# The token factor behind the gate and up matmuls, the shift as one more input column, in the last half FFN

## The chip, the cores and the metric

One core of a Trainium2 chip. TensorE does the matmuls, VectorE (DVE) and ScalarE (ACT) the elementwise work, GpSimd (POOL) some of it, SyncE (SP) starts the transfers. The metric is the device time of one execution in microseconds (us).

## The reference

Two blocks on 256 tokens of width 1024, in float32. The second has two layers; the last step of its second layer is a half FFN on the 256 latent tokens alone. In short:

```python
def half_ffn(t, m, j):
    h = modulate(rmsnorm_2(t, norm_g[l, j]), m[3 * j], m[3 * j + 1])
    return t + 0.5 * m[3 * j + 2] * swiglu(h, w_gate, w_up, w_down)

def rmsnorm_2(x, g):   # per token: x * rsqrt(mean(x * x) + eps) * g
def modulate(h, shift, scale):  return h * (1 + scale) + shift
def swiglu(h, w_gate, w_up, w_down):  return (silu(h @ w_gate) * (h @ w_up)) @ w_down
```

With r the token's factor rsqrt(mean(x * x) + eps), s = g * (1 + scale) per channel and b the shift per channel, the input is h = r * (x * s) + b. So h @ w = r * ((x * s) @ w) + (b @ w): a factor per token, and a constant per output channel. The FFN is 2816 wide. Ahead of it stands the retention layer, which ends with an output projection that is added to x.

## The kernel before, in words

Activations lie transposed: 128 channels on the partitions, tokens along the free axis, eight channel blocks (KB) for the width of 1024. Every float32 product is made of three matmuls on numbers rounded to fp32r (`mm3`, L488 to L491): high weight by high input, high weight by the input's rest, the weight's rest by high input. So each weight tile and each input has a high part and a rest (`wh`, `wl`; `hh`, `ho`; `ah`, `ao`).

Weights come in items of 1 MB by DMA into `raw`, and are split in units: ScalarE casts to `wh` (L388), VectorE subtracts to `wl` (L389). `Stream.get` (L404) hands out the next unit and then calls `ahead` (L400), which splits on until two units wait (AHEAD, L332); with `later=True` it does not. `wh` and `wl` have four buffers each.

The order is the program's: every engine takes its instructions as the code issues them (`manual_schedule`), so a split that `get` issues stands on ScalarE and VectorE between the elementwise work before and after it.

The retention's output projection (L1738 to L1755) runs in two halves of eight output blocks m. Each block is 24 matmuls of 256 columns, then a residual step on VectorE (L1750). In the second half ScalarE squares the new block (`square`, L662 to L671) and GpSimd or VectorE adds up the squares. After block 7 come the column sums (`norm_s`, L677 and L678), the factor (`norm_v`: L581 on VectorE, the power of -0.5 on GpSimd, L582), two transposes to get it along the free axis (`norm_b`, L694) and the copy to `Rb` (L701).

The last FFN is `ffn(1, 2, 1, None)`, one lane of N = 256 tokens. Its `start` makes the first two of its output blocks: for each channel block k `norm_u` (L710, `hu` = x * s * Rb) on VectorE, the shift and the split in `norm_h` (L722 to L727) on ScalarE, VectorE and GpSimd, and gate and up interleaved behind it. The other blocks go gate, then up: 24 matmuls each, Silu from PSUM on ScalarE (`act_in`, L1273), the product with up from PSUM on VectorE (`av`, L1278), the cast `ah` on ScalarE (L1279), the rest `ao` on VectorE (L1280). The FFN's width goes in two halves h of 11 blocks, 22 units each for gate and up; after each half the down projection: eight blocks of 33 matmuls, in units of 6 and 5 tiles (768 and 640 columns), each with a residual (L1353). PSUM has four banks (`pj`) for all of this.

Of the kernel before, what the change touches and what calls it, by code (L numbers as in the profile page):

```python
# [445 lines left out]
def build(tc, aps, stage=99):  # L446
# [4 lines left out]
    with ctx:  # L451
# [36 lines left out]
        def mm3(out, wh, wl, xh, xlo, first, last):  # L488
            pe.matmul(out, wh, xh, start=first, stop=False)  # L489
            pe.matmul(out, wh, xlo, start=False, stop=False)  # L490
            pe.matmul(out, wl, xh, start=False, stop=last)  # L491
# [188 lines left out]
        def norm_s(a):  # L680
            Z["ps", a] = ps = bank("at", "pss")
            sums(ps, 0, Z["ss"][:, LANE[a]], Z["sq", a])
# [20 lines left out]
        def norm_b(a):  # L703
            norm_t(a)
            norm_c(a)
# [552 lines left out]
        def ffn(l, j, lanes, nxt, first=0, ready=(), on_k=None, first_s=None, post=None):  # L1258
            N = 256 * lanes
            FF = ExitStack()  # L1260
            qp = FF.enter_context(tc.tile_pool(name=f"ffn{l}{j}", bufs=1, reuse_waits="tile"))
            if lanes == 1:
                skew = qp.tile([128, 48], F32, name="skew")
                pool.memset(skew, 0.0)
                Z["hh"] = qp.tile([128, KB, N], F32R, name="h1")
                Z["ho"] = qp.tile([128, KB, N], F32R, name="o1")
            hh, ho, gx = Z["hh"], Z["ho"], Z["gx"]
            ah = qp.tile([128, 11, N], F32R, name="ah")
            ao = qp.tile([128, 11, N], F32R, name="ao")

            def act_in(pg):
                sg = qp.tile([128, N], F32, name="sg", tag="sg", bufs=2)
                act.activation(sg, pg[:, :N], AF.Silu)  # L1273
                return sg

            def act_out(m, sg, pu):
                av = qp.tile([128, N], F32, name="av", tag="av", bufs=2)
                dve.tensor_tensor(av, sg, pu[:, :N], op=OP.mult)  # L1278
                act.copy(ah[:, m, :], av)  # L1279
                dve.tensor_tensor(ao[:, m, :], av, ah[:, m, :].bitcast(F32), op=OP.subtract)  # L1280

            def start():
                order = [first, 1 - first][:lanes]
                w, ps = [], [[bank("pj") for _ in range(2)] for _ in range(2)]
                done = {a: KB if a in ready else 0 for a in range(2)}
                done[0] = Z.pop("prep", 0)

                def prepare(a, k):
                    while done[a] <= min(k, KB - 1):
                        norm_h(l, j, done[a], a, first_s, a or done[a] % 2)  # L1290
                        done[a] += 1

                prepare(order[0], 1)
                for i, a in enumerate(order):
                    L = LANE[a]
                    for m in range(2):
                        if i == 0:
                            w.append([W.get(("gu", l, j, m), later=True) for _ in range(2)])
                        span = 1
                        for u, k in [(u, k0 + k) for k0 in range(0, KB, span) for u in range(2) for k in range(span)]:  # L1300
                            if m == u == 0:
                                prepare(a, k + 2)
                            s = slice(k * 128, (k + 1) * 128)
                            wh, wl = w[m][u]
                            mm3(ps[m][u][:, L], wh[:, s], wl[:, s], hh[:, k, L], ho[:, k, L], k == 0, k == KB - 1)
                            if u == 0:
                                continue
                            step = 8 * m + k
                            if i == 0 and lanes == 2:
                                if on_k:  # L1310
                                    on_k(step)
                                if step > 11:
                                    prepare(order[1], step - 12)
                            if i == 0 and step in ((2, 5) if lanes == 2 else (4, 7)) and len(W.split) < 2:
                                W.split_next()
                        if i == len(order) - 1:
                            act_out(m, act_in(ps[m][0]), ps[m][1])
                            if m == 0:
                                W.split_next()
                                W.split_next()  # L1320
                            else:
                                W.ahead()
                                if first_s:
                                    th.spawn(first_x())
                        if i or m or lanes == 1:
                            th.tick()

            for h in range(2):
                for m in range(11):
                    if h == 0 and m < 2:  # L1330
                        if m == 0:
                            start()
                        continue
                    key = ("gu", l, j, h * 11 + m)
                    for u in range(2):
                        wh, wl = W.get(key)
                        ps = bank("pj")
                        for k in range(KB):
                            s = slice(k * 128, (k + 1) * 128)
                            mm3(ps[:, :N], wh[:, s], wl[:, s], hh[:, k, :N], ho[:, k, :N], k == 0, k == KB - 1)  # L1340
                        if u == 0:
                            sg = act_in(ps)
                        else:
                            act_out(m, sg, ps)
                        th.tick()
# [203 lines left out]
        def retention():  # L1549
# [186 lines left out]
            derive_gate(1, 1)  # L1736
            derive_scale(1, 2)
            gh, go = G2["h"], G2["o"]  # L1738
            for khalf in range(2):
                if khalf == 1:  # L1740
                    th.drain()
                for m in range(KB):
                    wh, wl = W.get(("ro", khalf, m // 2), later=(khalf == 1 and m > KB - 3))
                    o = bank("pj")[:, :T]
                    for i in range(8):
                        s = slice(i * 128, (i + 1) * 128)
                        k = 8 * khalf + i
                        mm3(o, wh[:, s], wl[:, s], gh[:, k, :], go[:, k, :], i == 0, i == 7)
                    x = xl[:, m, :]
                    dve.scalar_tensor_tensor(x, o, gx[:, 1, 1, m, 0:1], x, op0=OP.mult, op1=OP.add)  # L1750
                    if khalf == 1:
                        square(m, 0)
                        if m == KB - 2:
                            W.split_next()
                    th.tick()  # L1755
            norm_s(0)
            norm_v(0)
            W.ahead()
            norm_b(0)
            RC.close()  # L1760
            RB.close()

# [53 lines left out]
```

## Time and profile before

| | |
|---|---|
| median of 3 runs | 2265.23 us (2263.64 to 2265.62) |
| the profiled execution | 2270.17 us, span 2268.4 us |
| TensorE matmuls, busy in the span | 2231.9 us (98%) |
| VectorE, ScalarE, GpSimd | 1428.7 (63%), 919.4 (41%), 179.2 us (8%) |
| mean granted TensorE clock | 0.995 |
| from the last output matmul of the retention to the end | from 2060.9 to 2268.4 us |

Times in the rows are us from the start of the span. A row of a group gives line, engine, operation, tiles (out<-in), shapes and count, then busy time and the mean ns of one, and what ended the idle time before. A row of the order in time gives start, duration, the same names, and in brackets the engine's idle time before and what ended it. PE is TensorE; a granted clock of 1.00 is 2.4 GHz.

### The profile page before, as it was taken

Reading aid. Unit: us, or ns where it says so; the run is one execution under the profiler, and the core shown is the slowest. Engines: PE = TensorE matmul, PEld = TensorE weight load, DVE = VectorE, ACT = ScalarE, POOL = GpSimd, SP = SyncE. Lnnn points to the kernel's source line nnn. Section 1 sums busy time; section 2 is a strip of 40 time slices with the busy share of each in tenths; the row PEclk is TensorE's granted clock in tenths of the full one; section 3 lists DMA queues with packets and bytes.
Section 4 is the critical chain, followed back from the end, with each engine's and each line's share of the span. In section 5 each row is a group of like instructions: output and inputs, shape, how many; then the busy total and the mean of one; then the engine's idle time right before and its main releaser. Section 6 shows DMA issues by size and latency. Waiting matters only on the chain.

```text
span 2268.4 us, 30969 instructions
## 1 busy us (share of the span) xinstructions
PE 2231.9 (98%) x12576; PEld 1907.8 (84%) x12576; DVE 1428.7 (63%) x2160; ACT 919.4 (41%) x1453; POOL 179.2 (8%) x207
## 2 busy tenths in 40 slices
PE   9999999999999999999999999999999999999998
PEld 7787887878888887898888888888888888899998
DVE  6776667766577766555666566556555656665554
ACT  5455444556432333454322334332232533335443
POOL 2100011012100000111000002000001100001001
PEclk9999999999999999999999999999999999999999
DMA  6444565445344554212445444344434423344553
GB/s 238 139 140 140 184 233 194 172 149 186 135 176 169 196 181 150 103 65 104 167 162 181 170 150 155 121 140 157 148 127 146 150 103 124 137 161 164 177 197 110
DMA packets 57167, 351.67 MB, mean 155 GB/s; under 512 B 6464, under 2 KB 6976, under 8 KB 23872
## 3 DMA queue, kind: packets, MB, share of 16 engines
q1 hardware_dynamic: 55872, 346.02, 43.5%
q10 hardware_dynamic: 1152, 3.67, 0.5%
q8 instruction: 98, 1.61, 0.3%
q14 instruction: 45, 0.37, 0.0%
HBM read 348.62 MB, written 1.05 MB: 154 GB/s over the span
## 4 chain that ended last, share of the span: by engine, by line
PE 87%; DVE 5%; ACT 3%; issue 2%; DMA 1%; POOL 1%; SPq 0%; DVEq 0%; ACTq 0%; POOLq 0%
PE pj L489 20%; PE pj L490 20%; PE pj L491 20%; PE pj L640 4%; PE pj L641 3%; PE pj L642 3%; DVE wl L389 2%; PE pj L1605 1%; PE pj L1607 1%; PE pj L1606 1%; ACT wh L388 1%; PE psc L933 1%; PE ada L527 1%; PE ppv L1061 1%; DMA raw<-w 1%
## 5 line engine op out<-in xcount | busy, mean ns | idle before, releaser
L389 DVE TENSOR_TENSOR wl<-raw,wh 128x1024 fp32r<-128x1024 f32 (+4 forms) x549 | 621.0, 1144 | 333.1 <-ACT wh L388 331.9
L388 ACT CAST wh<-raw 128x1024 fp32r<-128x1024 f32 (+4 forms) x549 | 520.7, 967 | 235.4 <-DMA raw<-w 145.6
L490 PE MATMUL pj<-ho,wh 128*128 128x512 f32 (+1 forms) x1280 | 465.6, 364 | 3.4 <-POOL ho L727 1.8
L489 PE MATMUL pj<-hh,wh 128*128 128x512 f32 (+1 forms) x1280 | 467.4, 365 | 0.5 <-ACT hh L722 0.4
L491 PE MATMUL pj<-hh,wl 128*128 128x512 f32 (+1 forms) x1280 | 464.3, 363 | 0.8 <-DVE wl L389 0.8
L489 PEld LDWEIGHTS pj<-hh,wh 128*128 128x128 f32 x1280 | 241.4, 189 | 45.6 <-ACT sg L1273 5.0
L516 DVE SCALAR_TENSOR_TENSOR acc<-raw,sc,acc 128x1024 f32<-128x1024 f32 x224 | 278.9, 1286 | 0.0
L490 PEld LDWEIGHTS pj<-ho,wh 128*128 128x128 f32 x1280 | 241.5, 189 | 42.8 <-POOL ho L727 3.4
L491 PEld LDWEIGHTS pj<-hh,wl 128*128 128x128 f32 x1280 | 241.5, 189 | 39.2 <-DVE wl L389 1.0
L489 PE MATMUL pj<-ah,wh 128*128 128x512 f32 (+1 forms) x770 | 268.7, 349 | 0.3 <-ACT wh L388 0.3
L491 PE MATMUL pj<-ah,wl 128*128 128x512 f32 (+1 forms) x770 | 266.8, 347 | 0.5 <-DVE wl L389 0.5
L490 PE MATMUL pj<-ao,wh 128*128 128x512 f32 (+1 forms) x770 | 266.7, 346 | 0.0
L640 PE MATMUL pj<-wh,xh 128*128 128x512 f32 (+2 forms) x480 | 191.4, 399 | 0.0
L641 PE MATMUL pj<-wl,xh 128*128 128x512 f32 (+2 forms) x480 | 184.7, 385 | 2.9 <-DVE wl L389 2.9
L642 PE MATMUL pj<-wh,xo 128*128 128x512 f32 (+2 forms) x480 | 183.7, 383 | 0.0
L1279 ACT CAST ah<-av 128x512 fp32r<-128x512 f32 (+1 forms) x88 | 49.9, 567 | 313.9 <-DVE av L1278 313.9
L489 PEld LDWEIGHTS pj<-ah,wh 128*128 128x128 f32 x770 | 145.0, 188 | 24.1 <-ACT wh L388 4.7
L491 PEld LDWEIGHTS pj<-ah,wl 128*128 128x128 f32 x770 | 145.8, 189 | 19.5 <-DVE wl L389 1.1
L490 PEld LDWEIGHTS pj<-ao,wh 128*128 128x128 f32 x770 | 145.1, 188 | 17.6
L670 POOL TENSOR_TENSOR ss<-ss,sq 128x256 f32<-128x256 f32 x55 | 48.6, 891 | 1308.6 <-ACT sq L668 1308.4
L1278 DVE TENSOR_TENSOR av<-sg,pj 128x512 f32<-128x512 f32 (+1 forms) x88 | 54.6, 620 | 149.5 <-PE pj L491 135.3
L1273 ACT ACTIVATE sg<-pj 128x512 f32<-128x512 f32 (+1 forms) x88 | 47.8, 543 | 192.8 <-PE pj L491 192.6
(316 smaller groups left out, 3468.9 us busy)
## 6 DMA issues: line engine op xcount, KB each, us to landing
raw<-w SPq DMA_DIRECT2D x258, 1024.0 KB, 4.8
raw<-w SPq DMA_DIRECT2D x64, 704.0 KB, 4.1
raw<-w SPq DMA_DIRECT2D x16, 768.0 KB, 4.2
de<-decay SPq DMA_DIRECT2D x24, 256.0 KB, 4.5
raw<-w SPq DMA_DIRECT2D x4, 904.0 KB, 4.5
raw<-w SPq DMA_DIRECT2D x6, 512.0 KB, 3.7
mk<-masks ACTq DMA_DIRECT2D x2, 768.0 KB, 5.1
xl<-xt SPq DMA_DIRECT2D x4, 256.0 KB, 5.4
```

The costliest lines, as they stand in the source:

```text
L388: self.nc.scalar.copy(hi[:, d], r[:, o])
L389: (sub or self.nc.vector).tensor_tensor(lo[:, d], r[:, o], hi[:, d].bitcast(F32), op=OP.subtract)
L489: pe.matmul(out, wh, xh, start=first, stop=False)
L490: pe.matmul(out, wh, xlo, start=False, stop=False)
L491: pe.matmul(out, wl, xh, start=False, stop=last)
L516: dve.scalar_tensor_tensor(acc[:, r, :], w, s, acc[:, r, :], op0=OP.mult, op1=OP.add)
L640: pe.matmul(o, xh[:, k, ts], wh[:, s], start=(k == 0), stop=False)
L641: pe.matmul(o, xh[:, k, ts], wl[:, s], start=False, stop=False)
L642: pe.matmul(o, xo[:, k, ts], wh[:, s], start=False, stop=(k == KB - 1))
L670: (dve if k == KB - 2 else pool).tensor_tensor(d, d, q, op=OP.add)
L1278: dve.tensor_tensor(av, sg, pu[:, :N], op=OP.mult)
L1279: act.copy(ah[:, m, :], av)
```

## The change

Only the FFN with one lane changes. `hh` is now x * s alone, made block by block in the retention's second output half (`act.activation` with the scale, and the rest `ho` on VectorE), in the middle 256 columns (48 to 304) of the tiles that the two-lane FFNs use. Two more columns (304, 305) hold the shift, so that each of the 1056 gate and up matmuls has 258 columns. `late` takes each result from PSUM: `nt` is the result times `Rb`, `nb` the column of the shift. Gate: Silu of `nt` with `nb` as bias. Up: (`nt` + `nb`) * Silu in one VectorE step. `start` isn't called for one lane any more: all blocks go gate, then up. The norm's sums and factor are issued after the first gate (`norm_r(0)`), the transposes and the copy to `Rb` after the first up (`norm_b(0)`); the gate result waits in its bank until then. In the retention the two places that held splits back (`later`) or issued them by hand are gone.

```diff
             if lanes == 1:
                 skew = qp.tile([128, 48], F32, name="skew")
                 pool.memset(skew, 0.0)
-                Z["hh"] = qp.tile([128, KB, N], F32R, name="h1")
-                Z["ho"] = qp.tile([128, KB, N], F32R, name="o1")
-            hh, ho, gx = Z["hh"], Z["ho"], Z["gx"]
+                hh, ho = hh[:, :, 48:306], ho[:, :, 48:306]
+            NI = hh.shape[-1]
...
+            def late(ps):
+                t = qp.tile([128, N], F32, name="nt", tag="nt", bufs=3)
+                b = qp.tile([128, 1], F32, name="nb", tag="nb", bufs=4)
+                dve.tensor_tensor(t, ps[:, :N], Z["Rb"][:, :N], op=OP.mult)
+                dve.tensor_copy(b, ps[:, N:N + 1])
+                return t, b
+
             def act_in(pg):
                 sg = qp.tile([128, N], F32, name="sg", tag="sg", bufs=2)
-                act.activation(sg, pg[:, :N], AF.Silu)
+                if lanes == 1:
+                    t, b = late(pg)
+                    act.activation(sg, t, AF.Silu, bias=b)
+                else:
+                    act.activation(sg, pg[:, :N], AF.Silu)
                 return sg
 
             def act_out(m, sg, pu):
                 av = qp.tile([128, N], F32, name="av", tag="av", bufs=2)
-                dve.tensor_tensor(av, sg, pu[:, :N], op=OP.mult)
+                if lanes == 1:
+                    t, b = late(pu)
+                    dve.scalar_tensor_tensor(av, t, b, sg, op0=OP.add, op1=OP.mult)
+                else:
+                    dve.tensor_tensor(av, sg, pu[:, :N], op=OP.mult)
...
-                    if h == 0 and m < 2:
+                    if h == 0 and m < 2 and lanes == 2:
...
-                            mm3(ps[:, :N], wh[:, s], wl[:, s], hh[:, k, :N], ho[:, k, :N], k == 0, k == KB - 1)
+                            mm3(ps[:, :NI], wh[:, s], wl[:, s], hh[:, k], ho[:, k], k == 0, k == KB - 1)
+                        if lanes == 1 and h == m == 0:
+                            if u == 0:
+                                norm_r(0)
+                                pg = ps
+                                continue
+                            norm_b(0)
+                            sg = act_in(pg)
...
             gh, go = G2["h"], G2["o"]
+            X = slice(48, 304)
+            for i in (304, 305):
+                act.copy(hh[:, :, i:i + 1], mods[:, 1, 48:56, 0:1])
+                dve.tensor_tensor(ho[:, :, i:i + 1], mods[:, 1, 48:56, 0:1], hh[:, :, i:i + 1].bitcast(F32),
+                                  op=OP.subtract)
...
-                    wh, wl = W.get(("ro", khalf, m // 2), later=(khalf == 1 and m > KB - 3))
+                    wh, wl = W.get(("ro", khalf, m // 2))
...
                     dve.scalar_tensor_tensor(x, o, gx[:, 1, 1, m, 0:1], x, op0=OP.mult, op1=OP.add)
                     if khalf == 1:
+                        g = Z["sp"][:, 1, 2, m, 0:1]
+                        act.activation(hh[:, m, X], x, AF.Copy, scale=g)
+                        dve.scalar_tensor_tensor(ho[:, m, X], x, g, hh[:, m, X].bitcast(F32),
+                                                 op0=OP.mult, op1=OP.subtract)
                         square(m, 0)
-                        if m == KB - 2:
-                            W.split_next()
                     th.tick()
-            norm_s(0)
-            norm_v(0)
-            W.ahead()
-            norm_b(0)
```

## Rows read from the trace of the kernel before

**Rows 1.** The page: span, and the first line of busy times.
```profile
span 2268.4 us, 30969 instructions
PE 2231.9 (98%) x12576; PEld 1907.8 (84%) x12576; DVE 1428.7 (63%) x2160; ACT 919.4 (41%) x1453; POOL 179.2 (8%) x207
```
**Rows 2.** Busy time by stretch: length, engines in turn, clock, DMA share, GB/s.
```profile
2061.00:2064.00 3.00, 1.09 (x10) 0.92 (x8) 1.57 (x4) 1.35 (x2) 0.28 (x1) 1.00 0.20 82
2064.00:2067.00 3.00, 0.43 (x2) 0.19 (x2) 1.51 (x3) 0.58 (x2) 1.43 (x2) 0.85 0.37 87
2067.00:2070.00 3.00, 2.65 (x10) 2.39 (x11) 2.64 (x7) 2.51 (x7) 1.31 (x2) 0.50 0.62 262
2079.00:2100.00 21.00, 21.00 (x181) 21.00 (x180) 12.56 (x16) 9.80 (x16) 0.00 (x0) 1.00 0.54 183
...
12.00:18.00 6.00, 5.01 (x21) 3.47 (x19) 5.16 (x9) 4.33 (x9) 3.28 (x2) 1.00 1.01 404
```
**Rows 3.** TensorE in order of time, around the gap.
```profile
2058.14 0.28 PE L491 MATMUL pj<-gh,wl 128*128 128x256 f32 x1
...
2060.86 0.28 PE L491 MATMUL pj<-gh,wl 128*128 128x256 f32 x1
...
2063.08 0.36 PE L678 MATMUL pss<-ones,sq 128*128 128x2 f32 x2
2065.40 0.43 PE L694 MATMUL prb<-ident,r 128*128 128x128 f32 x2 [1.96 <-POOL r L582]
2067.36 0.58 PE L489 MATMUL pj<-h,wh 128*128 128x256 f32 x1 [1.52 <-ACT h L722]
```
**Rows 4.** VectorE in order of time, residuals of the retention's second output half.
```profile
2042.14 0.48 DVE L1750 SCALAR_TENSOR_TENSOR xl<-pj,gx,xl 128x256 f32<-128x256 f32 x1 [1.10 <-PE pj L491]
...
2057.50 0.48 DVE L1750 SCALAR_TENSOR_TENSOR xl<-pj,gx,xl 128x256 f32<-128x256 f32 x1
...
2061.57 0.48 DVE L1750 SCALAR_TENSOR_TENSOR xl<-pj,gx,xl 128x256 f32<-128x256 f32 x1
```
**Rows 5.** ScalarE in order of time, behind the first of these residuals.
```profile
2042.66 0.42 ACT L665 ACTIVATE ss<-xl 128x256 f32<-128x256 f32 x1 [3.49 <-DVE xl L1750]
2042.98 1.03 ACT L388 CAST wh<-raw 128x1024 fp32r<-128x1024 f32 x1
```
**Rows 6.** VectorE in order of time, gate and up of the last FFN.
```profile
2087.23 0.42 DVE L1278 TENSOR_TENSOR av<-sg,pj 128x256 f32<-128x256 f32 x1 [0.19 <-PE pj L491]
...
2092.88 0.42 DVE L1278 TENSOR_TENSOR av<-sg,pj 128x256 f32<-128x256 f32 x1 [0.19 <-PE pj L491]
...
2094.73 1.22 DVE L389 TENSOR_TENSOR wl<-raw,wh 128x1024 fp32r<-128x1024 f32 x1 [0.53 <-ACT wh L388]
...
2132.45 0.42 DVE L1278 TENSOR_TENSOR av<-sg,pj 128x256 f32<-128x256 f32 x1 [0.91 <-PE pj L491]
```
**Rows 7.** ScalarE in order of time, the table load and the first Silu.
```profile
2074.90 1.28 ACT L1273 ACT_TABLE_LOAD   x1
2076.20 0.38 ACT L1273 ACTIVATE sg<-pj 128x256 f32<-128x256 f32 x1
```
**Rows 8.** ScalarE in order of time, gate and up: the cast of `av`, then a weight's.
```profile
2087.68 0.41 ACT L1279 CAST ah<-av 128x256 fp32r<-128x256 f32 x1 [1.90 <-DVE av L1278]
2087.99 1.04 ACT L388 CAST wh<-raw 128x1024 fp32r<-128x1024 f32 x1
```
**Rows 9.** Groups by line and form, VectorE, whole span: busy us, mean ns.
```profile
L1117 DVE TENSOR_TENSOR gt<-pj,Rbh 128x256 f32<-128x256 f32 x16 | 6.7, 418 | 1.3 <-PE pj L491 1.2
...
L802 DVE SCALAR_TENSOR_TENSOR xl<-xl,small,Rb 128x256 f32<-128x256 f32 x8 | 3.8, 476 | 0.0
...
L581 DVE TENSOR_SCALAR rv<-pss 128x2 f32<-128x2 f32 x14 | 2.2, 156 | 9.7 <-PE pss L678 9.7
```
**Rows 10.** Groups by line and form, ScalarE, whole span.
```profile
L725 ACT ACTIVATE hu<-hu,mods 128x256 f32<-128x256 f32 x45 | 22.7, 505 | 11.7 <-DVE hu L710 11.7
...
L1439 ACT ACTIVATE hh<-xl,sp 128x256 fp32r<-128x256 f32 x8 | 4.0, 494 | 0.0
```

More of the change, by code (lines that the diff above doesn't have):

```diff
@@ L1261, in ffn @@
             qp = FF.enter_context(tc.tile_pool(name=f"ffn{l}{j}", bufs=1, reuse_waits="tile"))
+            hh, ho, gx = Z["hh"], Z["ho"], Z["gx"]
             if lanes == 1:
@@ L1282, in start @@
             def start():
-                order = [first, 1 - first][:lanes]
+                order = [first, 1 - first]
                 w, ps = [], [[bank("pj") for _ in range(2)] for _ in range(2)]
@@ L1308, in start @@
                             step = 8 * m + k
-                            if i == 0 and lanes == 2:
+                            if i == 0:
                                 if on_k:
@@ L1313, in start @@
                                     prepare(order[1], step - 12)
-                            if i == 0 and step in ((2, 5) if lanes == 2 else (4, 7)) and len(W.split) < 2:
+                            if i == 0 and step in (2, 5) and len(W.split) < 2:
                                 W.split_next()
@@ L1324, in start @@
                                     th.spawn(first_x())
-                        if i or m or lanes == 1:
+                        if i or m:
                             th.tick()
```

## The prediction

> **What bounds the kernel now.** I read the page first, then a table of stretches around the end of the retention and the last FFN, then the order of work of each engine there. The page [rows 1]: matmuls for 98% of a span of 2268.4 us. So any change has to show up as matmul time, or as time in which TensorE waits. The table [rows 2]: from 2061 to 2067 TensorE does almost nothing (1.09 and 0.43 us busy of 3), and from 2067 to 2070 it runs at a granted clock of 0.50 (1.2 GHz instead of 2.4). That is the gap the change aims at: the last output matmul of the retention starts at 2060.86, the first gate matmul of the FFN at 2067.36 [rows 3]. From 2079 on TensorE is full, while VectorE is busy for 12.56 us of 21 and ScalarE for 9.80: neither is near saturation.
>
> Busy shares don't tell the whole story. VectorE and ScalarE hand work to each other, each in the program's order, and the length of that hand-over chain is what has to be compared with TensorE's pace. In the retention's second half it is already longer. TensorE needs 2.72 us for an output block (24 matmuls, 2058.14 to 2060.86 [rows 3]), but the residual steps L1750 go from 2042.14 to 2057.50 in five steps, 3.07 us each [rows 4]: residual, square on ScalarE, the cast `wh` behind it on ScalarE (starts 0.32 after the square [rows 5]), the difference `wl` on VectorE, next residual. It falls behind and costs nothing only because the weights are split two units ahead and there are just eight blocks. In gate and up the pace is 5.65 us for 48 matmuls (`av` at 2087.23 and 2092.88 [rows 6], 0.1177 each), and the hand-overs still wait for TensorE, not TensorE for them.
>
> **The change, part by part.**
>
> Removed: in the gap, the norm's chain stands between the last residual and the first gate matmul, then `hu`, shift, split for eight blocks. This goes; but see when the new `hh` is ready.
>
> Retention, second half. Each block gets `hh` on ScalarE between residual and square, and `ho` on VectorE. Nearest row for `hh`: L1439, same form, 0.494 us [rows 10]; a ScalarE instruction starts about 0.10 before its predecessor ends (2042.66 + 0.42 against 2042.98 [rows 5]), so 0.40 is added to the chain. `ho`, 0.48 by L802 [rows 9], runs while ScalarE squares and casts: free. The step becomes 3.47, and the residual of block 7 comes at 2042.14 + 7 x 3.47 = 2066.4, not 2061.57 [rows 4]. Gate's last two matmuls need `hh` and `ho` of that block: 0.48 + 0.04 + 0.49 + 0.04 + 0.48, at 2067.9; they end at 2068.35. The rest of gate 0 is done by then. The two shift columns, four tiny instructions ahead of the output blocks, are hidden by the retention's matmuls; without that cover they cost under 1 us.
>
> First block. The sums, four pairs of small matmuls (one pair 0.36, overlapping, 0.9 in all [rows 3]), then up 0, 24 x 0.1177: its end E(0) is 2072.1. Before, the same 48 matmuls were through at about 2075.7 (from 2067.36, about 24 at the half clock, 256 columns at 1.2 GHz or 0.213 each, the rest at 0.113). So 3.6 us are gained here, not the 6.5 of the gap and the half clock behind it. The square root runs behind up 0. Then the transposes (0.43 [rows 3]), the copy to `Rb` (0.38, as the Silu of that size [rows 7]), the table load, which used to stand beside matmuls (1.28 at 2074.90, Silu at 2076.20 [rows 7]), and the Silu: the first `av` at 2074.6.
>
> Gate and up. This is where I expect the loss. Each of the 44 results gets two instructions on VectorE: `nt`, 0.418 by L1117, the same form [rows 9], and `nb`, one column, 0.156 by L581. `av` becomes a three-operand step with a column, 0.476 by L802 [rows 9]. Silu gets a column as bias: 0.505 by L725 against 0.384 [rows 10, 7]. More important: Silu no longer reads TensorE's result, it waits for VectorE; and VectorE has the previous `wl` ahead of `nt`. So one loop closes, all in program order. Latencies from start to start (the next on the same engine 0.10 early on ScalarE [rows 5] and, an estimate, 0.08 on VectorE; 0.04 after the end where a result is handed over, as 2042.14 + 0.48 to 2042.66 [rows 4, 5]):
> - after up: `nt` 0.34, `nb` 0.16 + 0.04, `av` 0.48 + 0.04, `ah` 0.31, cast 1.04 + 0.04, `wl` 1.14: 3.59 [rows 6, 8, 9]
> - after gate: `nt` 0.34, `nb` 0.16 + 0.04, Silu 0.41, cast 1.04 + 0.04, `wl` 1.14: 3.17.
>
> 6.75 per block against TensorE's 5.65. Splitting runs two units ahead, which buys some 2 us, so after two or three blocks TensorE waits for `wl`.
> - First half: `av` of block 10 at 2074.6 + 10 x 6.75 = 2142.1, less 1.4 because the last splits are of 768 and 640 columns, not 1024 (estimate, by columns): 2140.7. `ao` is there 1.40 later, and the first down block's last three matmuls end 0.56 after that: 2142.7. Before: `av` of block 10 at 2132.45 [rows 6], 33 matmuls of 0.1177 behind it: 2136.3. Late by 6.4. The second down block then waits for its late split, 0.7 (its cast stands behind the last `ah`).
> - Second half, starting level: 10 x (6.75 - 5.65) + 0.53 - 1.4 + 1.40 + 0.56 - 3.88 = 8.2, and 0.7 again.
>
> Two more columns per matmul, 1056 of them: the trace has no 258-column matmul. The same 256 columns ran at 0.113 and at 0.1177, so columns alone don't set the pace; between nothing and 258/256 (0.9 ns each, 1 us in all), I take nothing, as TensorE waits in most of these blocks anyway. The Trainium skill (TensorE: Matmul & The Clock Gate, Back-to-back issue gap) gives a gap of N/2.4 plus a constant, 0.83 ns more per matmul; the sum would be up to 0.9 us higher.
>
> The table load shows Silu starting 0.02 after it [rows 7]. The Trainium skill (ScalarE: Activation LUTs, What ACT_TABLE_LOAD costs) has another 1.38 us of drain behind each, which speaks against having it on the path; by that the sum would be 1.4 higher. No sign of it in the row, and it is left out.
>
> **Sum.** 6.4 + 0.7 + 8.2 + 0.7 = 16.0 us slower. The profiled execution took 2270.17 us (span 2268.4 and 1.8 around it), so 2286.2; the median of the runs shown is 2265.23, 4.9 lower, so 2281.2.
>
> Bounds. Low: `nb` at 0.08, Silu at 0.384, `av` at 0.418, `hh` at the square's 0.42: 6.4 per block, about 8.5 in all. High: each of the three new steps waits 0.06 to 0.1 longer, 7.0 per block, and the half clock (0.213) is still granted for some 3 us around 2068: about 24. So 2273.7 to 2289.
>
> **The rivals.**
> - The hand-overs stay covered (10%): the change brings what its gap offers. It decides at 6.75 against 5.65: the 1.1 us between them is the whole of `nt`, `nb` and the longer Silu and `av`, so they would have to cost next to nothing, or the engines would have to run past a waiting instruction. Against it: in the retention the same kind of chain already runs at its own length [rows 4]. Then only the transition counts: 3.6 us with the 3.47 step; without it the last residual stays at 2061.57, its `hh` and `ho` at 2063.1, up 0 ends near 2067.3, 8.4 earlier than 2075.7. That is 2257 to 2262, faster.
> - The clock falls (6%): with TensorE waiting a sixth of the time, half clock in gate and up; 48 x 0.213 = 10.2 per block; over a third of the 22 blocks 7 x 4.6, some 25 to 30 more: 2305 to 2312. For it: clock 0.50 after 2061 to 2067 [rows 2]. Against: 5.01 of 6 us busy kept 1.00 at the start [rows 2], and 5.65 of 6.75 is the same share.
> - The chain binds only partly (4%), 6 us or less per block: loss and gain cancel, 2263 to 2270. Here also falls the case that the new operands let TensorE run at 0.113 rather than 0.1177.
>
> **The numbers.** The forecast 80%: its own range 2273.7 to 2289. The range is 2272 to 2290, taking in a little of the partial case. About 0.2%, 4.5 us, is what a measurement of this kernel can tell from no change. Faster 0.10 (the first rival), same 0.04 (most of the third), slower 0.86 (forecast and second).
>
> **What would show it.** Right: `av` about 6.7 us apart in the middle of each half; TensorE idle before L491 and L489, released by `wl` and `wh` (L389, L388); VectorE's idle time there ended by ScalarE and the other way round, hardly by TensorE; the residuals in the retention 3.4 to 3.5 apart; down blocks still 3.88. Wrong: `av` at 5.65 to 5.7, with `nt` waiting for TensorE. Granted clock under 1 between 2080 and 2220 would be the second rival.

## The result and the profile after

The changed kernel takes 2288.2 us (median of four runs, 2285.2 to 2289.3), the kernel before 2264.4 beside it (2261.3 to 2265.6): a ratio of 1.0095, 95% interval 1.0078 to 1.0113. It is slower, as forecast, by 23.8 us, where the forecast had 16.0 against 2265.2.

Two profiles of the kernel before show its last FFN at two TensorE paces (113.3 and 117.7 ns a matmul; fifth experiment), and the profile ahead of the prediction caught the slower one.

The page of the changed kernel, its span and busy times [rows 1]:

```profile
span 2287.5 us, 31096 instructions
PE 2244.2 (98%) x12576; PEld 1912.2 (84%) x12576; DVE 1446.9 (63%) x2246; ACT 920.1 (40%) x1451; POOL 173.9 (8%) x203
```

The busy shares are those of before, to within a point. They tell nothing of the loss. Busy time by stretch, the columns as in [rows 2]:

```profile
2061.00:2064.00 3.00, 2.57 (x22) 2.37 (x22) 1.92 (x3) 1.53 (x3) 0.57 (x1) 1.00 0.33 63
2064.00:2067.00 3.00, 2.56 (x22) 2.37 (x21) 2.16 (x4) 1.31 (x4) 0.25 (x2) 1.00 0.68 287
2067.00:2070.00 3.00, 1.17 (x11) 0.97 (x9) 2.00 (x4) 1.31 (x3) 0.00 (x0) 1.00 0.13 16
...
2073.00:2076.00 3.00, 3.00 (x16) 3.00 (x16) 0.57 (x1) 0.00 (x0) 1.14 (x1) 0.51 0.42 115
2079.00:2100.00 21.00, 20.22 (x160) 19.38 (x160) 12.77 (x26) 8.93 (x14) 0.00 (x0) 1.00 0.30 105
```

The gap is filled as intended: 2.57 and 2.56 us of matmuls where there were 1.09 and 0.43. A rest of it has moved to 2067, and half clock (0.51) now falls into the first up result. In the long stretch TensorE does 160 matmuls in 21 us where it did 181, at full clock, while VectorE is hardly busier than before (12.77 us against 12.56) and ScalarE less. Who waits for whom shows in the order of time on VectorE: the first and last residual of the retention's second half, the first product (the `av` step, one for each block), one turn of gate and up, and the last product of the first half [rows 4, 6]:

```profile
2044.72 0.48 DVE L1777 SCALAR_TENSOR_TENSOR xl<-pj,gx,xl 128x256 f32<-128x256 f32 x1 [1.10 <-PE pj L491]
...
2068.85 0.48 DVE L1777 SCALAR_TENSOR_TENSOR xl<-pj,gx,xl 128x256 f32<-128x256 f32 x1
...
2078.72 0.48 DVE L1291 SCALAR_TENSOR_TENSOR av<-nt,nb,sg 128x256 f32<-128x256 f32 x1 [0.94 <-ACT sg L1282]
...
2111.97 0.42 DVE L1274 TENSOR_TENSOR nt<-pj,Rb 128x256 f32<-128x256 f32 x1
2112.31 0.15 DVE L1275 COPY nb<-pj 128x1 f32<-128x1 f32 x1
2112.49 0.49 DVE L1291 SCALAR_TENSOR_TENSOR av<-nt,nb,sg 128x256 f32<-128x256 f32 x1
2113.45 0.42 DVE L1295 TENSOR_TENSOR ao<-av,ah 128x256 fp32r<-128x256 f32 x1 [0.47 <-ACT ah L1294]
2114.41 1.23 DVE L389 TENSOR_TENSOR wl<-raw,wh 128x1024 fp32r<-128x1024 f32 x1 [0.53 <-ACT wh L388]
2115.55 0.42 DVE L1274 TENSOR_TENSOR nt<-pj,Rb 128x256 f32<-128x256 f32 x1
2115.88 0.15 DVE L1275 COPY nb<-pj 128x1 f32<-128x1 f32 x1
2117.60 1.22 DVE L389 TENSOR_TENSOR wl<-raw,wh 128x1024 fp32r<-128x1024 f32 x1 [1.57 <-ACT wh L388]
2118.74 0.42 DVE L1274 TENSOR_TENSOR nt<-pj,Rb 128x256 f32<-128x256 f32 x1
...
2145.12 0.48 DVE L1291 SCALAR_TENSOR_TENSOR av<-nt,nb,sg 128x256 f32<-128x256 f32 x1
```

And on ScalarE: the table load with the first Silu [rows 7], then the same turn [rows 8]:

```profile
2076.88 1.28 ACT L1282 ACT_TABLE_LOAD   x1
2078.18 0.51 ACT L1282 ACTIVATE sg<-nt,nb 128x256 f32<-128x256 f32 x1
...
2113.01 0.41 ACT L1294 CAST ah<-av 128x256 fp32r<-128x256 f32 x1 [2.21 <-DVE av L1291]
2113.33 1.05 ACT L388 CAST wh<-raw 128x1024 fp32r<-128x1024 f32 x1
2116.12 0.51 ACT L1282 ACTIVATE sg<-nt,nb 128x256 f32<-128x256 f32 x1 [1.75 <-DVE nb L1275]
2116.54 1.03 ACT L388 CAST wh<-raw 128x1024 fp32r<-128x1024 f32 x1
```

Follow the brackets round: VectorE waits for the cast `wh`, the cast stands behind Silu or `ah`, these wait for VectorE's `nb` or `av`, which stand behind VectorE's `wl`. In this turn no bracket of VectorE or ScalarE names TensorE. From `nt` of up at 2111.97 to `nt` of gate at 2115.55 are 3.58 us, from there to the next 3.19: a turn of 6.77. The waits of TensorE and of ScalarE from 2080 to 2140 say the same (engine, line and whom it waited for; us in total, times, longest):

```profile
PE pj L491 <- DVE wl L389: 3.1, 8, 0.4
...
ACT ah L1294 <- DVE av L1291: 17.7, 8, 2.2
ACT sg L1282 <- DVE nb L1275: 15.7, 9, 1.8
```

In the kernel before TensorE waited for no `wl` here. Its first product stands at:

```profile
2076.61 0.42 DVE L1278 TENSOR_TENSOR av<-sg,pj 128x256 f32<-128x256 f32 x1 [0.47 <-ACT sg L1273]
```

The loss by stretch, from the starts of residuals and products in three profiles, two of the kernel before and one of the changed kernel (us; "last residual" is the last one of the retention's first output half, whose code the change leaves as it is):

| stretch | before, 117.7 ns | before, 113.3 ns (fifth experiment) | changed |
|---|---|---|---|
| start of the last residual | 2039.42 | 2039.20 | 2042.00 |
| last residual to first product | 37.19 | 37.46 | 36.72 |
| first half, first to last product | 55.84 | 54.18 | 66.40 |
| down, to the next product | 36.75 | 35.36 | 35.54 |
| second half, first to last product | 56.53 | 54.40 | 66.41 |
| to the end | 42.64 | 41.46 | 40.44 |
| sum of the five stretches | 228.96 | 222.86 | 245.52 |

So the changed kernel loses 16.6 us against the slower pace and 22.7 against the other; all of it, and a little more, lies in the two gate and up halves.

### The profile page after: what moved, and what is told of

Its sections match the earlier page's. It is cut to its first block, busy times and chain, and to the rows that moved or that the text cites. A ratio compares the mean times of both kernels' runs of the same rounds, so it can differ in the third digit from the quotient of the medians.

```text
span 2287.5 us, 31096 instructions
## 1 busy us (share of the span) xinstructions
PE 2244.2 (98%) x12576; PEld 1912.2 (84%) x12576; DVE 1446.9 (63%) x2246; ACT 920.1 (40%) x1451; POOL 173.9 (8%) x203
## 4 chain that ended last, share of the span: by engine, by line
PE 81%; DVE 9%; ACT 5%; issue 3%; DMA 1%; POOL 1%; SPq 0%; DVEq 0%; ACTq 0%; POOLq 0%
PE pj L489 18%; PE pj L491 18%; PE pj L490 18%; DVE wl L389 4%; PE pj L640 4%; PE pj L641 3%; PE pj L642 3%; ACT wh L388 3%; PE pj L1629 1%; PE pj L1628 1%; PE pj L1627 1%; PE psc L933 1%; PE ada L527 1%; PE ppv L1061 1%; DMA raw<-w 1%
## 5 line engine op out<-in xcount | busy, mean ns | idle before, releaser
L491 PE MATMUL pj<-hh,wl 128*128 128x512 f32 (+2 forms) x1632 | 568.0, 348 | 7.3 <-DVE wl L389 6.8
L489 PE MATMUL pj<-hh,wh 128*128 128x512 f32 (+2 forms) x1632 | 568.2, 348 | 2.3 <-ACT hh L1780 1.8
L490 PE MATMUL pj<-ho,wh 128*128 128x512 f32 (+2 forms) x1632 | 566.4, 347 | 3.5 <-POOL ho L727 1.9
L491 PEld LDWEIGHTS pj<-hh,wl 128*128 128x128 f32 x1632 | 309.3, 190 | 52.0 <-DVE wl L389 13.7
L489 PEld LDWEIGHTS pj<-hh,wh 128*128 128x128 f32 x1632 | 309.2, 189 | 47.8 <-ACT sg L1284 4.2
L490 PEld LDWEIGHTS pj<-ho,wh 128*128 128x128 f32 x1632 | 309.3, 190 | 42.9 <-POOL ho L727 3.4
L1293 DVE TENSOR_TENSOR av<-sg,pj 128x512 f32<-128x512 f32 x66 | 45.4, 687 | 143.0 <-PE pj L491 130.1
L640 PEld LDWEIGHTS pj<-wh,xh 128*128 128x128 f32 x480 | 91.1, 190 | 29.7 <-issue 7.0
```

Source lines behind the costliest of these rows:

```text
L640: pe.matmul(o, xh[:, k, ts], wh[:, s], start=(k == 0), stop=False)
```

## The experiments

Times are medians with their range; "before" is the kernel before on the same chip. They keep their numbers but stand in the order in which they explain each other.

**1. The waits meant to go, the work left.** In `act_in` and `act_out`:

```diff
-                    act.activation(sg, t, AF.Silu, bias=b)
+                    act.activation(sg, pg[:, :N], AF.Silu, bias=mods[:, 1, 48, 0:1])
...
-                    dve.scalar_tensor_tensor(av, t, b, sg, op0=OP.add, op1=OP.mult)
+                    dve.scalar_tensor_tensor(av, pu[:, :N], mods[:, 1, 48, 0:1], sg, op0=OP.add, op1=OP.mult)
```

> The changed kernel, but Silu and the product read TensorE's result again instead of what VectorE made of it (both with a column that lies ready for the shift, so their forms stay). The two new VectorE instructions per result are still issued and take their time; nothing reads what they write, so the token factor and the shift are left out of the computation. Theory (a closed loop of hand-overs): the loop is open, so the products come 5.65 to 5.85 us apart again instead of 6.77, TensorE hardly waits for a weight split, and only the transition counts: 2257 to 2265 us, 23 to 30 below the changed kernel. Rival (load: VectorE has simply too much to do in a block): VectorE's work per block is the same, so the products stay 6.5 to 6.8 apart and the time stays at 2283 or above. Rival (columns: 258 columns cost TensorE the time): the same, no change against the changed kernel.

Measured: 2284.57 us (2283.84 to 2285.90; before 2265.66), products 6.62 apart. That is what the rivals expected, and taken by the total alone it would have buried the theory. The order of time on ScalarE says why it doesn't:

```profile
2111.60 0.48 ACT L1282 ACTIVATE sg<-pj,mods 128x256 f32<-128x256 f32 x1 [1.77 <-DVE nb L1275]
```

Silu reads nothing that `nb` writes, and still it waits 1.77 us for `nb`. Both read the same result in PSUM, and in this program as built the read issued later waits for the one issued before it (the sixth experiment turns the order round, and the wait goes). So the wait was not taken away, and the run doesn't test the loop; it shows only that a turn is 0.15 us shorter when Silu and the product read PSUM.

**6. The same, with the two instructions issued behind Silu.** What comes off in the first experiment is the data, here also the order:

```diff
-                    t, b = late(pg)
-                    act.activation(sg, t, AF.Silu, bias=b)
+                    act.activation(sg, pg[:, :N], AF.Silu, bias=mods[:, 1, 48, 0:1])
+                    late(pg)
```

> As the first experiment (Silu and the product read TensorE's result; token factor and shift are left out), but the two VectorE instructions on a gate result are issued behind its Silu, so that Silu waits for TensorE alone. VectorE's and ScalarE's work per block is that of the first experiment to the instruction. Theory (closed loop): the loop is now 5.0 us (the second cast runs beside the two VectorE instructions), under TensorE's 5.80, so the products are 5.80 apart and the time is that of the reordered kernel: 2268 to 2274. Rival (load): products 6.6 apart as in the first experiment, 2284.

Measured: 2271.63 us (2268.21 to 2274.23; before 2265.37). Silu on ScalarE and two products on VectorE, in order of time:

```profile
2101.23 0.47 ACT L1281 ACTIVATE sg<-pj,mods 128x256 f32<-128x256 f32 x1 [0.69 <-PE pj L491]
...
2104.47 0.48 DVE L1291 SCALAR_TENSOR_TENSOR av<-pj,mods,sg 128x256 f32<-128x256 f32 x1
...
2110.27 0.48 DVE L1291 SCALAR_TENSOR_TENSOR av<-pj,mods,sg 128x256 f32<-128x256 f32 x1
```

Silu waits for TensorE, and the products are 5.80 apart. VectorE has the same instructions as in the first experiment: the load rival falls. The first three products (2077.63, 2082.60, 2087.58) even show the new loop's own length, 4.97 and 4.98 us, while TensorE was still ahead: 5.0 had been worked out.

**2. The two columns alone,** in the kernel before:

```diff
-                Z["hh"] = qp.tile([128, KB, N], F32R, name="h1")
-                Z["ho"] = qp.tile([128, KB, N], F32R, name="o1")
+                Z["hh"] = qp.tile([128, KB, N + 2], F32R, name="h1")
+                Z["ho"] = qp.tile([128, KB, N + 2], F32R, name="o1")
...
-                            mm3(ps[:, :N], wh[:, s], wl[:, s], hh[:, k, :N], ho[:, k, :N], k == 0, k == KB - 1)
+                            mm3(ps[:, :NI], wh[:, s], wl[:, s], hh[:, k], ho[:, k], k == 0, k == KB - 1)
```

> The kernel before, with nothing changed but that the gate and up matmuls take 258 columns instead of 256 (the two more are written once and nobody reads their results). Theory: 1056 matmuls at 0 to 3 ns more each, 0 to 3.3 us in all, so 2264 to 2268. Rival (columns): 258 leaves a faster mode of the matmul or of the result's store, 10 us or more.

Measured: 2273.47 us (2271.10 to 2275.04; before 2265.66), ratio 1.0029 (1.0018 to 1.0041): 7.8 us by the medians and 6.6 by the ratio, about twice what was expected at most, and less than the rival's 10. Two products in the middle:

```profile
2096.50 0.42 DVE L1282 TENSOR_TENSOR av<-sg,pj 128x256 f32<-128x256 f32 x1 [0.27 <-PE pj L491]
...
2102.31 0.42 DVE L1282 TENSOR_TENSOR av<-sg,pj 128x256 f32<-128x256 f32 x1 [0.27 <-PE pj L491]
```

5.81 for 48 matmuls are 121 ns each. Against 117.7 that is the 3 ns expected, against 113.3 it is 7.5, and 1056 x 7.5 ns = 7.9 us, which fits the medians.

**3. Splits three units ahead.** The changed kernel with one line more, `W.AHEAD = 3 if lanes == 1 else 2`.

> The changed kernel with the weights of the last FFN split three units ahead instead of two. Theory: a unit more of slack (2.8 us) delays the first wait in each half but leaves the loop its length: products still 6.7 to 6.8 apart, some 2 to 3 us less per half, 4 to 6 in all: 2282 to 2285. Rival (late splits: TensorE waits only because the split is begun too late): a third unit ahead removes the waits, products 5.65 to 5.9 apart, 2265 to 2272.

Measured: 2288.17 us (2287.16 to 2290.43): nothing. Products are 6.77 apart from the second on, so the late-splits rival falls. The 4 to 6 us were a mistake in the expectation: slack delays TensorE's first wait, but not the hand-overs. They run at their own length from the first product (2078.64) to the last but two, whatever TensorE has in store, and the first down block of each half needs the last product. TensorE only stands still there instead:

```profile
2143.00:2146.00 3.00, 0.38 (x1) 0.19 (x1) 2.29 (x6) 1.05 (x3) 0.00 (x0) 1.00 0.52 205
2146.00:2149.00 3.00, 2.97 (x15) 2.97 (x16) 2.88 (x5) 1.51 (x3) 0.00 (x0) 0.56 0.35 81
```

It waits up to 2.7 us for `ah`, and the next 3 us have a granted clock of 0.56. The 0.9 us by which the two halves are shorter (65.96 and 65.92) are lost again in the down blocks.

**4. The split issued behind the new instructions.**

```diff
                     t, b = late(pg)
+                    W.ahead()
                     act.activation(sg, t, AF.Silu, bias=b)
...
                     dve.scalar_tensor_tensor(av, t, b, sg, op0=OP.add, op1=OP.mult)
+                    W.ahead()
...
-                        wh, wl = W.get(key)
+                        wh, wl = W.get(key, later=lanes == 1)
...
```

> The changed kernel, all of its arithmetic kept, with one thing reordered in gate and up: the next unit's weight split is issued behind the two new VectorE instructions (and the product) and ahead of Silu and of the copy to the high part, instead of ahead of the unit's matmuls. So the cast no longer stands behind a Silu that waits for VectorE, and the difference no longer stands ahead of the instructions that Silu waits for. Theory: the loop now runs once around per block in about 4 us, under TensorE's 5.65 to 5.85, so TensorE sets the pace: products 5.7 to 5.9 apart, 2257 to 2266, faster than the changed kernel by 22 to 30 and as fast as the kernel before or up to 8 faster. Rival (load, or the new operands themselves): VectorE and ScalarE have the same work, so products stay 6.5 or more apart, 2280 or above.

Measured: 2271.25 us (2267.13 to 2272.54; before 2265.66), 17 below the changed kernel. VectorE in order of time:

```profile
2101.22 0.43 DVE L1274 TENSOR_TENSOR nt<-pj,Rb 128x256 f32<-128x256 f32 x1 [1.28 <-PE pj L491]
...
2102.22 1.22 DVE L389 TENSOR_TENSOR wl<-raw,wh 128x1024 fp32r<-128x1024 f32 x1
...
2104.12 0.43 DVE L1274 TENSOR_TENSOR nt<-pj,Rb 128x256 f32<-128x256 f32 x1 [0.35 <-PE pj L491]
...
2107.02 0.43 DVE L1274 TENSOR_TENSOR nt<-pj,Rb 128x256 f32<-128x256 f32 x1 [1.28 <-PE pj L491]
```

`nt` waits for TensorE again, `wl` for nobody, and a block takes 5.80 (2101.22 to 2107.02), TensorE's own time for 48 matmuls of 258 columns. This is the whole change with all its arithmetic; order alone is worth 17 us. It comes out 5 us above the end of the range that was expected, 2257 to 2266, which had been reckoned from the slower pace of before (5.65 a block). Against the control's profile (fifth experiment) the two halves are longer by 5.5 us (56.04 and 58.00 against 54.18 and 54.40), about what is left over before (5.6 us by the medians): a block takes 5.80 where the control has 5.44, the two columns of the second experiment.

**5. The kernel before against itself.**

> The kernel before, unchanged, timed against itself: how far two sets of runs of one program differ, and a second profile of it. Expected: a ratio within 0.1% of 1. In the second profile the stretch from the first residual of the retention's second half to the end takes 229 us as in the first (228.96), whatever the total is. If that stretch is 4 us shorter or more, differences of this stretch between profiles don't stand for the difference of the medians.

Measured: 2267.50 us over twelve runs, six of them from 2262.5 to 2265.5 and six from 2269.5 to 2273.2; ratio 1.0009 (0.9995 to 1.0022). The new profile (2263.85 us) has the stretch at 222.86, not the 229 that was expected: 6.1 us shorter, with nothing changed. Two products:

```profile
2092.76 0.42 DVE L1278 TENSOR_TENSOR av<-sg,pj 128x256 f32<-128x256 f32 x1
...
2098.20 0.42 DVE L1278 TENSOR_TENSOR av<-sg,pj 128x256 f32<-128x256 f32 x1
```

5.44 for 48 matmuls, 113.3 ns each, where [rows 6] have 5.65. In the profile ahead of the prediction the matmuls of up 0 also stand 113 ns apart, until 2076.18; four spacings of 117 to 122 follow, and from there on all 1,500 or so to the end, down blocks too, stand 118 apart. In this profile they stay at 113.

**8. Other addresses,** in the kernel before: the tiles `ah` and `ao` allocated ahead of `h1` and `o1` instead of behind them.

> The kernel before, with nothing changed but the order in which the last FFN's tiles are laid into SBUF: the down matmuls' operands ahead of the gate and up matmuls' ones, so that all of them start at other addresses. In the kernel before a down block takes 3.88 us (117.7 ns a matmul), in the changed kernel 3.74 (113.4), though its down part is the same. Theory A (addresses): the paces change, down to 113.4 ns or gate and up to another than 117.7, the total by 2 us or more. Theory B (the pace hangs on how TensorE comes into the stage): paces and time as before.

Measured: 2264.43 us (2262.23 to 2271.79), ratio 0.9996 (0.9986 to 1.0007), profile at 113.3 ns throughout. With the control at 113.3 on the old addresses this tells neither of the two theories right: the pace isn't fixed by addresses, since one program shows both, but whether they make the slower one rarer (one of twelve runs above 2268 here, six of the control's twelve, ten of the 35 runs of before beside both) stays open.

**7. The same reordering in the retention,** on top of the fourth experiment:

```diff
-                    wh, wl = W.get(("ro", khalf, m // 2))
+                    wh, wl = W.get(("ro", khalf, m // 2), later=khalf == 1)
...
                     if khalf == 1:
+                        if m < KB - 1:
+                            W.ahead()
                         g = Z["sp"][:, 1, 2, m, 0:1]
...
                         square(m, 0)
+                        W.ahead()
```

> The reordered kernel (splits behind the two new VectorE instructions), with the same reordering in the retention's second half: the next split is issued behind the residual and ahead of the new high part, low part and square (behind them for the last block). Theory: the residuals are then 2.72 to 2.85 apart (TensorE's pace) instead of 3.445, the last one comes 4 to 5 us earlier, TensorE waits less ahead of the last two matmuls of the first gate result, and 3 to 5 us of the total go: 2266 to 2268, the stretch from the first of these residuals to the end 223 to 225 us (228.25 without it). Rival (this stretch is bounded by something else, the sums and the square root): under 1.5 us.

Measured: 2264.96 us (2262.78 to 2268.15; before 2265.37), ratio 0.9991 (0.9981 to 1.0001), 6.3 below the fourth experiment, where 3 to 5 had been expected. The first and last residual of the second half:

```profile
2044.50 0.48 DVE L1780 SCALAR_TENSOR_TENSOR xl<-pj,gx,xl 128x256 f32<-128x256 f32 x1 [2.24 <-PE pj L491]
...
2063.54 0.48 DVE L1780 SCALAR_TENSOR_TENSOR xl<-pj,gx,xl 128x256 f32<-128x256 f32 x1 [0.37 <-PE pj L491]
```

Seven steps in 19.04 us, 2.72 each, TensorE's own; the changed kernel took 24.13 (2044.72 to 2068.85). TensorE no longer stands still ahead of the last matmuls of gate 0, and no half clock follows. The change as a whole is now level with the kernel before: against the control's profile the first product comes 5.6 us sooner after the last residual (31.84 against 37.46), and the two halves take 5.5 us more. The filled gap pays for the columns.

**9 and 10. 256 columns, in the changed kernel and in the seventh experiment's.**

```diff
-                hh, ho = hh[:, :, 48:306], ho[:, :, 48:306]
+                hh, ho = hh[:, :, 48:304], ho[:, :, 48:304]
...
-                dve.tensor_copy(b, ps[:, N:N + 1])
+                dve.tensor_copy(b, ps[:, N - 1:N])
```

> The changed kernel with 256 columns in the gate and up matmuls; the one-column copy reads the last token's column instead, so the shift is left out of the computation and every instruction but the matmuls' width stays. Theory (closed loop): TensorE waits for the loop, so what it does in between costs nothing: products still 6.77 apart, the time within 1.5 us of the changed kernel's 2288.2. Rival (the 7.5 ns that two more columns take against 113.3 are what the change costs): 1056 of them, 8 us less, about 2280.

> The kernel reordered in both places, with 256 columns as in the run beside it (the shift is left out of the computation). Here TensorE sets the pace, so the columns should show: at 113.3 ns a matmul 7.9 us less than 2264.96, 2257, and products 5.44 apart; where TensorE comes into the slower of its two paces, 117.7 ns, 3.3 us less, 2261.7, and products 5.65 apart. Rival (the reordered kernel's pace is set by its hand-overs, not by the matmuls): products 5.8 apart, 2265.

Measured: 2288.80 us (2286.62 to 2289.43) for the ninth, two products of it:

```profile
2103.69 0.48 DVE L1291 SCALAR_TENSOR_TENSOR av<-nt,nb,sg 128x256 f32<-128x256 f32 x1
...
2110.47 0.48 DVE L1291 SCALAR_TENSOR_TENSOR av<-nt,nb,sg 128x256 f32<-128x256 f32 x1
```

Still 6.78 apart: in the changed kernel the columns cost nothing, since TensorE waits anyway. The tenth: 2263.65 us (2253.76 to 2265.13; before 2264.93), two products of it:

```profile
2097.87 0.48 DVE L1292 SCALAR_TENSOR_TENSOR av<-nt,nb,sg 128x256 f32<-128x256 f32 x1
...
2103.53 0.49 DVE L1292 SCALAR_TENSOR_TENSOR av<-nt,nb,sg 128x256 f32<-128x256 f32 x1
```

5.65 to 5.66, TensorE's slower pace; two of its twelve runs came out at 2253.8 and 2256.0, near the 2257 that belong to 113.3, ten from 2260.9 up. So once the loop is open TensorE sets the pace in gate and up. The total is only 1.3 us below the seventh experiment's 2264.96, where 3.3 had been expected at this pace: in its profile the down blocks have the slower pace too, 3.88 each where the seventh's have 3.74, and 16 of them give back 2.2 us.

**11. Only the first five blocks late.** On top of the seventh: blocks 0 to 4 of the first half take the raw input, `late` and 258 columns; one piece of the normalised input is made behind each result (`norm_h` into new tiles `h1`, `o1`), and from block 5 on gate and up read that.

```diff
...
+                    if lanes == 1 and h == 0 and m == 5:
+                        raw_h, hh, ho, NI = False, Z["hh"], Z["ho"], N
...
+                        if raw_h and len(nk) < KB:
+                            norm_h(l, j, len(nk), 0, spare=len(nk) % 2)
+                            nk.append(0)
...
```

> The kernel reordered in both places, but only the first five gate and up blocks of the first half take the raw input, the factor on their results and the 258 columns; meanwhile the normalised and shifted input is made for the rest, one 128-row piece per result, and the other 17 blocks run as in the kernel before with 256 columns. All of the computation is kept. Theory: the gap stays filled, and 17 blocks of 48 matmuls save 7.5 ns each, 6.1 us, less up to 1 us where VectorE has a piece more to do in the first five: 2259 to 2261, faster than the kernel before by 4 to 6 us. Rival (VectorE can't take the pieces beside the new instructions): products over 6.5 apart in blocks 1 to 4, which gives back 3 us or more: 2262 to 2265.

Measured: 2260.61 us (2257.71 to 2262.00; before 2264.93), ratio 0.9975 (0.9965 to 0.9986): faster than both kernels. One step of it went wrong. TensorE's waits from 2060 to 2100, and busy time by stretch:

```profile
PE pj L491 <- DVE wl L389: 0.7, 1, 0.7
PE pj L489 <- ACT wh L388: 0.7, 1, 0.7
```

```profile
2075.00:2078.00 3.00, 1.59 (x9) 1.38 (x10) 2.85 (x8) 2.87 (x5) 0.81 (x1) 0.92 0.31 128
2078.00:2081.00 3.00, 3.00 (x16) 3.00 (x16) 2.51 (x5) 1.75 (x3) 0.00 (x0) 0.51 0.22 33
```

Behind block 1 the split of the next unit stands behind the first normalised piece, TensorE is busy for 1.59 us of 3, and the next 3 us go by at a granted clock of 0.51 (1.2 GHz).

**12. The same, with `W.AHEAD = 3` in this FFN.**

> The kernel with the first five blocks on the raw input, with the weights of the last FFN split three units ahead. In the run without this, TensorE waited 0.72 and 0.75 us for the split of unit 4 behind block 1 (the cast stood behind the first normalised piece on ScalarE), and the granted clock fell to 0.51 for the block behind it: 1.4 us of waits and some 2.7 us of half clock. Theory: the third split is made in ScalarE's idle time before the factor is there, TensorE no longer waits and the clock stays at 1.00: 3 to 4 us less, 2256 to 2258. Rival (VectorE is behind for good in these blocks): the wait only moves a block later, 2259 to 2261.

Measured: 2257.03 us (2254.28 to 2258.52; before 2264.85), ratio 0.9958 (0.9943 to 0.9973). The same two stretches:

```profile
2075.00:2078.00 3.00, 3.00 (x27) 3.00 (x26) 2.85 (x8) 2.90 (x5) 0.81 (x1) 1.00 0.08 22
2078.00:2081.00 3.00, 3.00 (x27) 3.00 (x27) 3.00 (x8) 1.78 (x4) 0.00 (x0) 1.00 0.84 319
```

No wait and no half clock: 3.6 us. A unit more of slack does nothing against a loop that is too long (third experiment) and all that is needed against one late split. This version is 7.8 us faster than the kernel before and 31 faster than the changed one.

## Why the prediction was right, and by how much it was off

The forecast case came: slower, 2288.2 in a range of 2272 to 2290, by the mechanism named. Its steps in turn, in the profile of after (whose last residual of the first half stands 2.58 us later than before's, so 2.58 is taken off where a time of before was predicted):

- **Retention, 3.47 a step:** 24.13 / 7 = 3.45. The last residual was predicted at 2066.4; 2068.85 less 2.58 is 2066.3. Right; the seventh experiment shows the loss was avoidable.
- **First block:** the first product at 2074.6 predicted, 2078.72 less 2.58 = 2076.1 measured. Off by 1.5, for the half clock fell on up 0 (16 of its 24 matmuls of 258 columns at 0.214 instead of 0.12). It was priced in the high bound and left out of the sum.
- **Table load on the path:** Silu starts 0.02 us after its end at 2078.16. The Trainium skill (ScalarE: Activation LUTs, What ACT_TABLE_LOAD costs) has 1.38 us of drain in addition to a load; here, with nothing between load and Silu, none shows, as in the row of before.
- **The loop, 3.59 + 3.17 = 6.75:** 3.58 + 3.19 = 6.77. That it is the loop and not the load is shown by the fourth and sixth experiments: the same work per block, in another order, goes at 5.80. Split slack is no part of it (third). TensorE waits for `wl`, as said; for `wh`, which was also named, the table of waits has no row.
- **Columns at nothing:** right for this kernel (ninth experiment) and for the reason given, that TensorE waits anyway. Alone they cost 7.8 us by the medians (second), far above the bounds of nothing and 1 us: the 0.9 ns a matmul, in proportion to the columns, were 3 to 7.5 ns. The Trainium skill (TensorE: Matmul & The Clock Gate, Back-to-back issue gap) has N/2.4 + 2.5 ns as the gap of an isolated matmul at the full clock, by which two columns are an estimated 0.83 ns. The streams here show 3 to 7.5, so the 0.9 us worked out from it would have been as wrong.
- **Down blocks still 3.88:** no. In the changed kernel's profile they take 3.74, TensorE's faster pace:

```profile
2155.41 0.48 DVE L1375 SCALAR_TENSOR_TENSOR xl<-pj,gx,xl 128x256 f32<-128x256 f32 x1 [1.66 <-PE pj L491]
...
2174.11 0.48 DVE L1375 SCALAR_TENSOR_TENSOR xl<-pj,gx,xl 128x256 f32<-128x256 f32 x1 [0.99 <-PE pj L491]
```

Five steps in 18.70 us. In 16 down blocks that is 2.2 us less than reckoned.

- **The sum, 16.0 us against the profiled execution:** 245.52 - 228.96 = 16.6. That it comes so near is in part luck: the 1.5 us more in the first block and the 2.2 us less in the down blocks, neither of them in the sum, largely cancel.

**The step that failed in size is the last one,** "the median of the runs shown is 2265.23, 4.9 lower, so 2281.2". The 4.9 us between that profile and the median lay in TensorE's pace in this very FFN (228.96 against 222.86 in the control). The changed kernel can't keep that gain: its two halves take 66.4 us at whatever pace TensorE has, since the loop sets it (the ninth experiment has 66.47 in both, with 256 columns). So the sum should have stood on 2270.17. From there the two profiles differ by the stretch and by what lies ahead of it: 2270.17 + 16.56 + 2.58 = 2289.31, the profiled run of after. Those 2.58 us can't be put down to the change: 2.45 are there at 41 us, in code that is the same, and the other profiles differ there by 0.2 to 2.2 in no order that follows the kernels. Of the 7.0 us between 2281.2 and 2288.2, 4.9 are this step, 0.6 the sum, and the rest (2.6 less 1.1, by which the median of after lies under its profile) run to run. The median also lies just under the 2289 that the high bound gave, but not for that bound's reasons: it had 7.0 a block, and the loop measured 6.77.

The prediction's own text had the clue: it notes that the same 256 columns ran at 0.113 and 0.1177 in one trace, and uses it only to price the columns. Had it asked which of the two the median runs have, 5.44 would have stood for 5.65, and the loss at 10 x 0.21 more a half, besides the down blocks. A smaller slip: it is the last three matmuls of gate 0 that need the last block of `hh` and `ho`, not the last two.

The rivals: hand-overs staying covered is what the reordered kernels show (fourth and seventh); with both reorderings the time is 2265, so the 2257 to 2262 of this rival were too low, by what the columns cost (5.5 us). The clock is 1.00 in gate and up from 2079 on. A partly binding chain: no.

Open: what tips TensorE from 113 into 118 ns at 2076.18 in one run and not in another, and why 258 columns have 121 in every profile. Neither was tried further. The pace also changes within a run, and back: in the ninth experiment's profile the down blocks of the first half take 3.88 to 3.89, those of the second 3.74, both at a clock of 1.00. And that the two groups of times of the kernel before are the two paces rests on one profile in each.

## What to carry to other kernels

Busy shares don't bound a stage in which two engines hand work to each other in program order: write down the loop of hand-overs, add it up start to start, and compare it with the bottleneck's time per block. When an engine that read the bottleneck's result is made to wait for a third one, look at what that one has queued ahead, and issue independent work (here the next weight split) behind the new step and ahead of the waiting one; it was worth 17 us here, and a unit more of slack nothing (third experiment). And ask what makes one profile longer than the median before subtracting the difference: if it lies where the change takes over the pace, it doesn't carry over.

## What the runs showed of the hardware

- A stream of fp32r matmuls of 256 columns ran at 113.3 ns in one profile and at 117.7 in another of the same program, both at a granted clock of 1.00 (6 us of the total). In the one ahead of the prediction it went over to the slower at 2076.18 and stayed there to the end, some 180 us; in the ninth experiment's it was slower in the first half's down blocks and faster in the second's.
- 258 columns take 121 ns, 3 to 7.5 more than 256, in every profile that has them, where TensorE doesn't wait.
- ScalarE's read of a PSUM result waited 1.77 us for VectorE's read of the same result, issued ahead of it, with no data between them (first experiment); with the order turned round it waited for TensorE alone (sixth).
- With TensorE busy for 1.59 us of 3 the granted clock went to 0.51 for the next 3 us (eleventh experiment), and busy for 0.38 of 3 to 0.56 (third); short of work for about 1 us in every turn of 6.77 (6.77 less 48 x 0.121), in waits listed at 0.4 us or less, it kept 1.00.
